# Holding four vector sums behind a named sum, and another tile for one raw weight load, in a hybrid decoder layer

## The chip, the cores and the metric

The kernel runs on one core of a Trainium2 chip. The metric is the device time of one execution in microseconds (us); the median of the runs counts. TensorE (PE) multiplies, VectorE (DVE), ScalarE (ACT) and GpSimd (POOL) work on tiles, and transfers are issued from the queues of SyncE (SP) and of POOL. All products are single-precision, each made of three matmuls in fp32r over a high and a low half of both operands.

## The reference

One layer on 1024 tokens of width 1024. `r = x + mix(norm(x)) @ w_out`, where the mix is three groups of heads (a gated recurrence, a sliding window attention, a retention). Then the gated MLP with inner width 2816,

```
h2 = rmsnorm(r) * ffn_norm
gate = causal_conv3(h2 @ w_gate) + conv_b
r = r + (gelu(gate) * (h2 @ w_up)) @ w_down
r = r + (p @ w_ple_proj) * sigmoid((rmsnorm(r) * ple_norm) @ w_ple_gate)
out = rmsnorm(r) * final_norm
```

## The kernel before, in words

The attention part comes first (to about 400 us). It ends with the last gated heads, whose columns are scaled by the first norm, held in the tile `rs1` (tag `rs`, one buffer, in the pool that lives through the whole kernel). Then come the output projection and the projection of `p` (tiles `pp`), to 508 us.

The MLP's two products with `h2` are done in 22 *units* of 128 inner columns by a seven-product scheme (Strassen in Winograd's form): each unit needs products 1 to 7 instead of eight, on sums of quarters of the weights and of `h2`. One product is four blocks of three matmuls, twelve in all. `weights_up_1(f)` loads a unit's raw gate weights `wg` (512 KB, SP queue) and splits them into a high half (ACT, `whig`) and a low half (DVE, `wlog`); `weights_up_2(f)` loads the raw up weights `wu` and makes the sums `s12`, `f34`, `f4` with their halves. `Unit.early` makes products 1 and 2; for units 0, 1 and 2 these run before anything else, since they need only the plain `h2`. `Unit.rest` makes the others. It keeps three banks: `a` (product 2), `d` (5, then 3 on top) and `b` (1, 6, 7 and 4, one on top of the other). Between the products DVE and ACT read a bank before the next product adds to it: after product 7 `plus(u1, "b")` (L942, `us<-gb,us`) must have read bank `b` before product 4 writes it, with product 3 between; after product 3 `plus(g1, "d")` (L942, `gs<-gd,gs`) starts the convolution (L945 on ACT, L946 and L948 on DVE) on the tiles `gs` and `cv`, one buffer each.

Unit outputs go to DRAM from the POOL queue: an even unit stores `he` (L990), an odd one `ta`, `ho` and `tb` (L997 to L1001). `sent[f]` is the store after which `sums_down` may issue its load.

The down product is a seven-product scheme too. Its weight sums are made in 22 *pieces*, by `sums_down(n)`: a load of four 128x256 blocks from `w_dn` into tile `sd` (512 KB, POOL queue; tag `rs`, one buffer), four DVE operations (L1010 and three of L876, `sd<-sd`), a store to `s_dram` (POOL queue). Unit f (from 3 on) calls `sums_down(f - 3)`; pieces 19, 20 and 21 follow after the last unit.

The down phase runs seven passes in the order 1, 2, 6, 5, 7, 3, 4 of eleven steps each; a step is twelve matmuls, two steps share a group of raw weights `wdr` and four steps share raw activations `hr` (tag `hx`, six buffers), all loaded from the SP queue. Passes 1, 2 and 4 read `w_dn`, the others read `s_dram`. `residual(i)` loads two tiles of `r` (tag `hx` too, kept to the end); `gate_weights(d)` loads and splits `w_ple_gate` for the stage after it, the first three of them when a pass ends.

A planner orders the instructions of each engine before the run, from dependencies, priorities (`tc.high_priority` moves a block ahead) and estimated durations; on the chip every engine takes its instructions strictly in that order. `tc.issue_after(x)` puts the block's instructions of x's engine behind x in that order, without a wait of its own.

Of the kernel before, what the change touches and what calls it, by code (L numbers as in the profile page):

```python
# [17 lines left out]
F32 = mybir.dt.float32  # L18
# [4 lines left out]
ALU = mybir.AluOpType  # L23
# [3 lines left out]
P = 128  # L27
T = 1024
# [3 lines left out]
NF = 22  # L32
# [4 lines left out]
NJ = NF // 2  # L37
# [36 lines left out]
def trunk(ctx: ExitStack, tc: tile.TileContext, a, out, dbg):  # L74
    nc = tc.nc
    V, S, G, TE = nc.vector, nc.scalar, nc.gpsimd, nc.tensor

    cp = ctx.enter_context(tc.tile_pool(name="const", bufs=1))
# [14 lines left out]
    def half(h):  # L93
        return slice(h * H2, (h + 1) * H2)
# [31 lines left out]
    def col(i):  # L126
        return small[:, i:i + 1]
# [74 lines left out]
    with tc.high_priority(offset=100000):  # L202
# [4 lines left out]
        for k in range(KD):  # L207
            x = xs[k]
# [9 lines left out]
            for h in range(2):  # L218
                S.mul(hi[:, half(h)], x[:, half(h)], col(C_G1 + k))
                V.scalar_tensor_tensor(out=lo[:, half(h)], in0=x[:, half(h)], scalar=col(C_G1 + k),  # L220
                                       in1=hi[:, half(h)].bitcast(F32), op0=ALU.mult, op1=ALU.subtract)
# [480 lines left out]
    f, k = hgrn_f(0, first[0])  # L702
# [5 lines left out]
    f, k = got["af1"]  # L708
# [14 lines left out]
    for hd in range(2):  # L723
        r = slice(hd * 64, hd * 64 + 64)
# [33 lines left out]
    def f4(tag, name, shape=(P, T), dt=F32):  # L758
        if tag == "big":
            return big.tile(list(shape), dt, tag="big", name=name)  # L760
        if tag in ("wraw", "whi", "wlo"):
            return wp.tile(list(shape), dt, tag=tag, bufs=1 if tag == "wraw" else 2, name=name)
        return fp.tile(list(shape), dt, tag=tag, bufs=BUFS[tag], name=name)
# [29 lines left out]
    ho_dram, ta_dram, tb_dram = [dp.tile([NJ, P, T], F32, name=n) for n in ("hod", "tad", "tbd")]  # L793
# [3 lines left out]
    r = [f4("r", f"r{d}") for d in range(KD)]  # L797
# [77 lines left out]
    def minus(out, x, y):  # L875
        V.tensor_tensor(out=out, in0=x, in1=y, op=ALU.subtract)  # L876


    def weights_up_1(f):

        g = f4("ws" if f == 2 else "w5" if f > 2 and f % 2 else "wraw", f"wg{f}")
        nc.sync.dma_start(g.rearrange("p (k c) -> p k c", k=KD), a["w_gu"][f, 0])
        hi, lo = [f4(t, f"{t}g{f}", dt=F32R) for t in ("whi", "wlo")]
        hl(hi, lo, g)
        return g, {n + 1: (hi[:, half(n)], lo[:, half(n)]) for n in range(2)}
# [21 lines left out]
    class Unit:  # L907
# [21 lines left out]
        def rest(self):  # L929
            f, bank = self.f, self.bank  # L930
            gs, cv, us = [f4(t, f"{t}{f}") for t in ("gs", "cv", "us")]
            g0, g1 = [gs[:, half(i)] for i in range(2)]
            u0, u1 = [us[:, half(i)] for i in range(2)]

            def w(j):
                return col(C_CW + 3 * f + j)

            def copy(out, to):
                S.copy(out, bank[to])  # L939

            def plus(out, to):
                V.tensor_tensor(out=out, in0=bank[to], in1=out, op=ALU.add)  # L942

            def conv():
                S.activation(cv, gs, AF.Identity, bias=col(C_CB + f), scale=w(2))  # L945
                V.scalar_tensor_tensor(out=cv[:, 1:], in0=gs[:, :T - 1], scalar=w(1), in1=cv[:, 1:],  # L946
                                       op0=ALU.mult, op1=ALU.add)
                V.scalar_tensor_tensor(out=cv[:, 2:], in0=gs[:, :T - 2], scalar=w(0), in1=cv[:, 2:],  # L948
                                       op0=ALU.mult, op1=ALU.add)
                S.activation(cv, cv, AF.Gelu_apprx_tanh)  # L950

            if f < 3:
                copy(g0, "b")
                plus(g0, "a")
            if f == 0:
                self.prod(5)
                copy(u1, "d")
                self.prod(3)
                copy(g1, "d")
                self.prod(6)  # L960
                plus(g1, "b")
                conv()
                self.prod(7)
                plus(u1, "b")
            else:
                if f > 2:
                    s1 = fp.tile([P, H2], F32, tag="s1", bufs=1, name=f"s1{f}")
                    self.prod(1)
                    copy(s1, "b")
                    self.prod(5)  # L970
                    copy(u1, "d")
                self.prod(6)
                copy(g1, "b")
                if f > 2:
                    self.prod(2)
                    V.tensor_tensor(out=g0, in0=bank["a"], in1=s1, op=ALU.add)
                else:
                    self.prod(5)
                    copy(u1, "d")
                self.prod(7)  # L980
                plus(u1, "b")
                self.prod(3)
                plus(g1, "d")
                conv()
            self.prod(4)
            V.tensor_tensor(out=u0, in0=bank["b"], in1=cv[:, half(0)], op=ALU.mult)
            V.tensor_tensor(out=u1, in0=u1, in1=cv[:, half(1)], op=ALU.mult)
            j = f // 2
            if f % 2 == 0:
                sent[f] = G.dma_start(he_dram[j], u1)  # L990
                even.append(us)
                return
            e0, e1 = [even[j][:, half(i)] for i in range(2)]
            t1, t2 = [cv[:, half(i)] for i in range(2)]
            minus(t1, e0, e1)
            minus(t2, u0, t1)
            G.dma_start(ta_dram[j], cv)  # L997
            minus(e0, u0, e0)
            minus(e1, u1, t2)
            G.dma_start(ho_dram[j], us)  # L1000
            sent[f] = G.dma_start(tb_dram[j], even[j])  # L1001

    def sums_down(n):

        j, c = n // 2, slice(n % 2 * 256, n % 2 * 256 + 256)
        t = cp.tile([P, 4, 256], F32, tag="rs", bufs=1, name=f"sd{n}")
        with tc.issue_after(sent[min(n + 2, NF - 1)].ins):
            G.dma_start(t, a["w_dn"][:, j, :, c].rearrange("b p c -> p b c"))
        a11, a12, a21, a22 = [t[:, i, :] for i in range(4)]
        V.tensor_tensor(out=a22, in0=a21, in1=a22, op=ALU.add)  # L1010
        minus(a21, a11, a21)
        minus(a11, a22, a11)
        minus(a12, a12, a11)
        G.dma_start(s_dram[:, j, :, c].rearrange("b p c -> p b c"), t)

    even, sent = [], {}
# [34 lines left out]
    for f in range(3, NF):  # L1051
        with tc.high_priority(offset=3000):
            raw, A = weights_up_1(f)
            weights_up_2(f, raw, A)
        sums_down(f - 3)
        Unit(f, A).rest()


    for n in range(NF - 3, NF):
        sums_down(n)  # L1060
    steps = [(i, j) for i in DOWN for j in range(NJ)]
    raws = {}

# [33 lines left out]
    r = [None] * KD  # L1097
# [5 lines left out]
    def residual(i):  # L1103

        t = f4("hx", f"rr{i}", (P, 2, T))
        for d in (2 * i, 2 * i + 1):
            r[d] = t[:, d % 2, :]
            nc.sync.dma_start(r[d], r_dram[d])
        r2.append(t)
# [25 lines left out]
    def gate_weights(d):  # L1135
        with tc.high_priority(offset=300 if d > 2 else 0):
            raw = f4("us" if d < 3 else "ws" if d % 2 else "wraw", f"wpg{d}")
            nc.sync.dma_start(raw.rearrange("p (k c) -> p k c", k=KD), a["w_pg"][d])
            tags = ("whi", "wlo") if d in (3, 4) else ("big", "big")
            hi, lo = [f4(t, f"{c}pg{d}", dt=F32R) for t, c in zip(tags, "hl")]  # L1140
            hl(hi, lo, raw)
            wpg[d] = [x.rearrange("p (k c) -> p k c", k=KD) for x in (hi, lo)]
# [5 lines left out]
    bank = {}  # L1148
    todo = []
    for n, (i, j) in enumerate(steps):  # L1150
        if n % 2 == 0:
            got[n // 2] = parts(n // 2)
        if n in (4, 6, 12, 15):
            residual((4, 6, 12, 15).index(n))
        if n > 5 * NJ and todo or todo and j % 2:
            done(*todo.pop(0))
        (wh, wl), (xh, xl) = got[n // 2]
        to = "y" if i in (2, 5, 3) else "x"
        new = i in (1, 2, 5)
        if new and j == 0:  # L1160
            bank[to] = [(pg if (d < 2 if to == "y" else d == 0) else b1)(f"d{i}{d}") for d in range(4)]
        for d in range(4):
            mm3(bank[to][d], wh[:, n % 2, d * P:d * P + P], wl[:, n % 2, d * P:d * P + P], xh[:, n % 2, :],
                xl[:, n % 2, :], new and j == 0, j == NJ - 1, not new)
        if j == NJ - 1:
            d0, h = TO[i]
            for d in range(4):
                V.tensor_tensor(out=r[d0 + d][:, half(h)], in0=bank[to][d], in1=r[d0 + d][:, half(h)], op=ALU.add)
            if i in DONE:
                todo += [(DONE[i][0] + d, DONE[i][1]) for d in range(4)]  # L1170
            if i in (2, 6, 5):
                gate_weights((2, 6, 5).index(i))
    for x in todo:
        done(*x)
    for d in range(3, KD):
# [174 lines left out]
```

## Time and profile before

| | us |
|---|---|
| three runs | 1269.79, 1271.68, 1275.17 |
| median | 1271.68 |
| profiled execution, its span | 1272.79, 1270.8 |
| PE busy, DVE busy, ACT busy | 1236.2, 903.2, 551.7 |
| matmuls | 6198 |
| MLP units, about | 508 to 952 |
| down phase, about | 952 to 1160 |

The profiled execution is one of the program's executions; its span runs from the first to the last instruction. An idle stretch is shown in brackets with what ended it. The granted clock of TensorE is 1.00 at 2.4 GHz and 0.50 at 1.2 GHz; a mean between them says that a stretch had both.

### The profile page before, as it was taken

The numbers are of one execution on the slowest core, as the hardware profiler recorded it, in microseconds if no ns is written. First come the engines' busy times: TensorE is split into PE (matmuls) and PEld (weight loads), VectorE is DVE, ScalarE is ACT, GpSimd is POOL, SyncE is SP. The second block draws the span as 40 slices with busy tenths as digits, with TensorE's granted clock in tenths as the row PEclk, the third lists the DMA queues.
The fourth block names the chain that finished last, engine by engine and source line by source line (L and its number), as shares of the span: only waits on it lengthen the run. The fifth ranks groups of instructions, "written<-read, shape, count | busy, mean of one in ns | idle before, by whom it ended". The sixth has DMA issues, their size and how long they took to land. (4 is left out here: it accounts for less than half of the span.)

```text
span 1270.8 us, 16249 instructions
## 1 busy us (share of the span) xinstructions
PE 1236.2 (97%) x6198; PEld 1034.7 (81%) x6198; DVE 903.2 (71%) x1563; ACT 551.7 (43%) x856; POOL 130.2 (10%) x162
## 2 busy tenths in 40 slices
PE   9999999999999999999999999999999999999996
PEld 7888888888888888778787888888778778888896
DVE  7986967566776387787878778778573765665676
ACT  7324233248675355444433433343352343543432
POOL 2000000012210332000111110111101000000010
PEclk9999999999999999999999999999999999999998
DMA  7110110110103844223555444454689664543132
GB/s 253 50 32 19 34 34 18 34 50 18 34 18 104 311 133 158 91 92 124 186 179 166 154 170 132 158 174 156 217 289 348 227 235 162 164 139 100 42 109 83
DMA packets 61021, 165.02 MB, mean 130 GB/s; under 512 B 6096, under 2 KB 8656, under 8 KB 60944
## 3 DMA queue, kind: packets, MB, share of 16 engines
q1 hardware_dynamic: 43744, 106.44, 25.1%
q0 software_dynamic: 15616, 55.84, 12.9%
q10 hardware_dynamic: 1584, 1.71, 0.5%
q8 instruction: 48, 0.79, 0.2%
q14 instruction: 29, 0.24, 0.1%
HBM read 119.67 MB, written 44.30 MB: 129 GB/s over the span
## 5 line engine op out<-in xcount | busy, mean ns | idle before, releaser
L115 PE MATMUL d<-hhd,hwd 128*128 128x512 f32 x308 | 120.5, 391 | 2.5 <-ACT hwd L770 2.5
L117 PE MATMUL d<-hhd,lwd 128*128 128x512 f32 x308 | 120.8, 392 | 1.1 <-DVE lwd L771 1.1
L116 PE MATMUL d<-lhd,hwd 128*128 128x512 f32 x308 | 120.4, 391 | 0.0
L771 DVE TENSOR_TENSOR lwd<-wdr,hwd 128x1024 fp32r<-128x1024 f32 (+1 forms) x39 | 47.0, 1209 | 44.0 <-ACT hwd L770 43.9
L115 PE MATMUL gb<-b,hf 128*128 128x512 f32 x176 | 70.1, 399 | 5.6 <-DVE us L942 4.5
L770 ACT CAST hwd<-wdr 128x1024 fp32r<-128x1024 f32 (+1 forms) x39 | 40.3, 1038 | 78.7 <-PE d L116 63.5
L115 PEld LDWEIGHTS d<-hhd,hwd 128*128 128x128 f32 x308 | 58.2, 189 | 14.9 <-ACT hwd L770 2.9
L117 PE MATMUL gd<-b,f 128*128 128x512 f32 x176 | 68.3, 390 | 1.5 <-DVE f L771 1.5
L117 PEld LDWEIGHTS d<-hhd,lwd 128*128 128x128 f32 x308 | 58.2, 189 | 13.9 <-DVE lwd L771 1.9
L115 PE MATMUL gd<-b,f 128*128 128x512 f32 x176 | 68.8, 391 | 0.4 <-ACT us L939 0.2
L116 PE MATMUL gb<-b,hf 128*128 128x512 f32 x176 | 68.7, 390 | 0.0
L117 PE MATMUL gb<-b,lf 128*128 128x512 f32 x176 | 68.7, 390 | 0.0
L116 PE MATMUL gd<-b,f 128*128 128x512 f32 x176 | 68.5, 389 | 0.0
L116 PEld LDWEIGHTS d<-lhd,hwd 128*128 128x128 f32 x308 | 58.1, 189 | 12.1
L115 PE MATMUL pg<-hp,hpg 128*128 128x256 f32 (+1 forms) x192 | 61.7, 322 | 0.0
L116 PE MATMUL pg<-lp,hpg 128*128 128x256 f32 (+1 forms) x192 | 61.4, 320 | 0.0
L117 PE MATMUL pg<-hp,lpg 128*128 128x256 f32 (+1 forms) x192 | 61.2, 319 | 0.0
L770 ACT CAST hhd<-hr 128x1024 fp32r<-128x1024 f32 (+1 forms) x39 | 39.8, 1035 | 33.5 <-DMA hr<-tad 17.9
L771 DVE TENSOR_TENSOR lhd<-hr,hhd 128x1024 fp32r<-128x1024 f32 (+1 forms) x39 | 46.5, 1206 | 8.0 <-ACT hhd L770 7.8
L771 DVE TENSOR_TENSOR f<-s,f 128x1024 fp32r<-128x1024 f32 x22 | 26.9, 1225 | 33.5 <-ACT f L770 33.4
L770 ACT CAST f<-wg 128x512 fp32r<-128x512 f32 x22 | 13.7, 623 | 84.0 <-PE gd L117 84.0
L115 PEld LDWEIGHTS gb<-b,hf 128*128 128x128 f32 x176 | 33.0, 188 | 17.4 <-DVE us L942 7.7
(459 smaller groups left out, 3501.3 us busy)
## 6 DMA issues: line engine op xcount, KB each, us to landing
wu<-w_gu SPq DMA_DIRECT2D x22, 512.0 KB, 3.5
wg<-w_gu SPq DMA_DIRECT2D x22, 512.0 KB, 3.7
sd<-w_dn POOLq DMA_DIRECT2D x22, 512.0 KB, 5.2
sd<-sd POOLq DMA_DIRECT2D x22, 512.0 KB, 3.9
wdr<-sd SPq DMA_DIRECT2D x20, 512.0 KB, 4.2
wr_wo<-w_out SPq DMA_DIRECT2D x16, 512.0 KB, 3.7
wdr<-w_dn SPq DMA_DIRECT2D x15, 512.0 KB, 4.6
hod<-us POOLq DMA_DIRECT2D x11, 512.0 KB, 2.9
```

Source lines behind the costliest of these rows:

```text
L115: TE.matmul(o, wh, xh, start=first, stop=False, skip_group_check=on)
L116: TE.matmul(o, wh, xl, start=False, stop=False, skip_group_check=on)
L117: TE.matmul(o, wl, xh, start=False, stop=last, skip_group_check=on)
L770: S.copy(hi, src)
L771: e.tensor_tensor(out=lo, in0=src, in1=hi.bitcast(F32), op=ALU.subtract)
```

## The change

Unit 1's raw gate weights go to a tile with tag `rs` instead of `wraw`. `plus` returns its instruction; units 1 to 21 call `sums_down(f - 1, ...)` with the instruction of `plus(u1, "b")`, and the four DVE operations stand behind it in DVE's order. The load of piece n is issued after `sent[n]` instead of `sent[n + 2]`. The last piece, 21, is called at the end of the first pass of the down phase, behind the last addition to `r` there. An odd unit's `sent` is now the store of `ho` and not the one of `tb`. `residual` 1, 2 and 3 move from steps 6, 12 and 15 to steps 7, 22 and 26, and the first three `gate_weights` from the ends of passes 2, 6, 5 to those of 6, 5, 7.

```diff
 def weights_up_1(f):
-        g = f4("ws" if f == 2 else "w5" if f > 2 and f % 2 else "wraw", f"wg{f}")
+        if f == 1:
+            g = cp.tile([P, T], F32, tag="rs", bufs=1, name="wg1")
+        else:
+            g = f4("ws" if f == 2 else "w5" if f > 2 and f % 2 else "wraw", f"wg{f}")
...
                 self.prod(7)
-                plus(u1, "b")
+                sums_down(f - 1, plus(u1, "b"))
                 self.prod(3)
                 plus(g1, "d")
                 conv()
...
-            G.dma_start(ho_dram[j], us)
-            sent[f] = G.dma_start(tb_dram[j], even[j])
+            sent[f] = G.dma_start(ho_dram[j], us)
+            G.dma_start(tb_dram[j], even[j])
...
-    def sums_down(n):
+    def sums_down(n, after):
...
-        with tc.issue_after(sent[min(n + 2, NF - 1)].ins):
+        with tc.issue_after(sent[n].ins):
             G.dma_start(t, a["w_dn"][:, j, :, c].rearrange("b p c -> p b c"))
...
-        V.tensor_tensor(out=a22, in0=a21, in1=a22, op=ALU.add)
-        minus(a21, a11, a21)
-        minus(a11, a22, a11)
-        minus(a12, a12, a11)
+        with tc.issue_after(after.ins):
+            V.tensor_tensor(out=a22, in0=a21, in1=a22, op=ALU.add)
+            minus(a21, a11, a21)
+            minus(a11, a22, a11)
+            minus(a12, a12, a11)
         G.dma_start(s_dram[:, j, :, c].rearrange("b p c -> p b c"), t)
...
-        sums_down(f - 3)
         Unit(f, A).rest()
-    for n in range(NF - 3, NF):
-        sums_down(n)
...
-        if n in (4, 6, 12, 15):
-            residual((4, 6, 12, 15).index(n))
+        if n in (4, 7, 2 * NJ, 2 * NJ + 4):
+            residual((4, 7, 2 * NJ, 2 * NJ + 4).index(n))
...
-                V.tensor_tensor(out=r[d0 + d][:, half(h)], in0=bank[to][d], in1=r[d0 + d][:, half(h)], op=ALU.add)
+                x = V.tensor_tensor(out=r[d0 + d][:, half(h)], in0=bank[to][d], in1=r[d0 + d][:, half(h)], op=ALU.add)
+            if i == 1:
+                sums_down(NF - 1, x)
...
-            if i in (2, 6, 5):
-                gate_weights((2, 6, 5).index(i))
+            if i in (6, 5, 7):
+                gate_weights((6, 5, 7).index(i))
```

## Rows read from the trace of the kernel before

**Rows 1.** The first part of the page: busy time of each engine, its share of the span, instructions.

```profile
PE 1236.2 (97%) x6198; PEld 1034.7 (81%) x6198; DVE 903.2 (71%) x1563; ACT 551.7 (43%) x856; POOL 130.2 (10%) x162
```

**Rows 2.** The table by stretches: length; busy time of PE, its weight loads, DVE, ACT, POOL; granted clock; busy share of the DMA engines; GB/s. The stretches are the first half of the output projection, the preparation of the first units, units 0 to 2, the units in their steady run, the last two units, the first two passes.

```profile
400.00:450.00 50.00, 50.00 (x226) 41.30 (x225) 23.56 (x37) 16.37 (x20) 12.78 (x14) 1.00 0.76 268
...
489.00:535.00 46.00, 42.87 (x186) 34.88 (x185) 42.07 (x71) 27.32 (x44) 5.00 (x7) 0.96 0.38 133
535.00:600.00 65.00, 62.92 (x271) 50.00 (x270) 48.35 (x63) 28.58 (x34) 3.47 (x6) 1.00 0.36 114
...
700.00:900.00 200.00, 199.35 (x877) 164.02 (x876) 156.51 (x219) 78.52 (x93) 26.80 (x41) 1.00 0.47 154
900.00:960.00 60.00, 57.22 (x251) 46.75 (x251) 42.65 (x52) 26.13 (x29) 7.59 (x12) 1.00 0.83 296
960.00:1010.00 50.00, 49.46 (x219) 40.65 (x218) 25.39 (x32) 16.17 (x17) 3.79 (x5) 1.00 0.74 265
```

**Rows 3.** Who PE waited for between 420 and 1160 us, all of it: waiting line and what it waited for, us in total, times, longest.

```profile
PE gb L115 <- DVE us L942: 4.5, 4, 1.4
PE gb L115 <- ACT whig L770: 3.0, 1, 3.0
PE d L115 <- ACT hwd L770: 2.5, 1, 2.5
PE gd L117 <- DVE f L771: 1.5, 1, 1.5
PE d L117 <- DVE lwd L771: 1.1, 2, 0.5
PE gb L115 <- ACT gs L939: 0.7, 2, 0.5
PE gb L115 <- DVE gs L942: 0.4, 1, 0.4
PE gd L115 <- ACT us L939: 0.2, 1, 0.2
```

**Rows 4.** The timeline of PE around 517 us (start, duration), and the table by stretches for five us of it.

```profile
514.47 0.39 PE L117 MATMUL gb<-b,f 128*128 128x512 f32 x1
517.90 0.79 PE L115 MATMUL gb<-b,whig 128*128 128x512 f32 x1 [3.05 <-ACT whig L770]
...
521.19 0.39 PE L117 MATMUL gb<-b,wlog 128*128 128x512 f32 x1
...
515.00:520.00 5.00, 2.10 (x5) 1.71 (x6) 2.77 (x4) 2.51 (x3) 0.00 (x0) 0.74 0.06 24
```

**Rows 5.** The timelines of DVE, SP and ACT: the last reader of `rs1`, the last reader of unit 0's raw gate weights, the load of unit 1's, and the cast that waits for it.

```profile
384.05 0.68 DVE L281 TENSOR_TENSOR cg<-z_cg,rs 128x512 f32<-128x512 f32 x1
508.93 0.69 DVE L771 TENSOR_TENSOR f<-wg,f 128x512 fp32r<-128x512 f32 x1
509.65 0.33 SPq L882 DMA_DIRECT2D wg<-w_gu  x1
516.80 1.99 ACT L770 CAST whig<-wg 128x1024 fp32r<-128x1024 f32 x2 [2.56 <-DMA wg<-w_gu]
```

**Rows 6.** The tile `sd` by operation (duration in ns, least, median, most; first and last start), and DVE's waits for it between 540 and 1000 us.

```profile
L876 DVE TENSOR_TENSOR sd<-sd x66: 415/424/427, 600.3 to 1003.6; 128x256 f32<-128x256 f32 x66
DVE sd L1010 <- DMA sd<-w_dn: 32.8, 14, 10.2
```

**Rows 7.** The timelines of DVE and PE in one unit: the sums of a piece, the two `plus`, and product 3's first and last matmul with the first of product 4.

```profile
664.69 0.42 DVE L1010 TENSOR_TENSOR sd<-sd 128x256 f32<-128x256 f32 x1 [1.75 <-DMA sd<-w_dn]
668.16 0.42 DVE L876 TENSOR_TENSOR sd<-sd 128x256 f32<-128x256 f32 x1
669.10 0.69 DVE L942 TENSOR_TENSOR us<-gb,us 128x512 f32<-128x512 f32 x1
665.87 0.39 PE L115 MATMUL gd<-b,f 128*128 128x512 f32 x1
668.37 0.39 PE L117 MATMUL gd<-b,f 128*128 128x512 f32 x1
669.84 0.50 PE L115 MATMUL gb<-b,hf 128*128 128x512 f32 x1 [1.08 <-DVE us L942]
```

**Rows 8.** The chain of waits that ended last, in order of time (start, us, what), around 1000 us, and the timeline of PE there.

```profile
993.09 8.00 DMA sd<-w_dn
1001.21 0.42 DVE sd L1010
1008.59 0.36 SPq L1075
1009.00 8.31 DMA wdr<-sd
...
1015.55 0.39 PE L117 MATMUL d<-hhd,lwd 128*128 128x512 f32 x1
1018.43 0.50 PE L115 MATMUL d<-hhd,hwd 128*128 128x512 f32 x1 [2.49 <-ACT hwd L770]
1022.73 0.40 PE L115 MATMUL d<-hhd,hwd 128*128 128x512 f32 x1
```

**Rows 9.** The timelines of DVE and ACT: the last operation of a unit's convolution on DVE, and the next unit's write to the same tile `gs`.

```profile
654.17 1.28 DVE L948 SCALAR_TENSOR_TENSOR cv<-gs,small,cv 128x1022 f32<-128x1022 f32 x1
661.59 0.58 ACT L939 COPY gs<-gb 128x512 f32<-128x512 f32 x1
```

More of the change, by code (lines that the diff above doesn't have):

```diff
@@ L941, in plus @@
             def plus(out, to):
-                V.tensor_tensor(out=out, in0=bank[to], in1=out, op=ALU.add)
+                return V.tensor_tensor(out=out, in0=bank[to], in1=out, op=ALU.add)
             def conv():
```

## The prediction

> **What bounds the kernel now.** I began with the busy times: PE has work in 97% of the span [rows 1], so the other engines matter only where PE stands still, and of the 34.6 us in which it does (1270.8 less 1236.2) I had to find those that the change can touch. The list of PE's waits over the MLP and down phases answers that [rows 3]: eight lines, 13.9 us together. They fall into four places. First, unit 1's gate weights (`whig`), 3.05 us in one piece. Second, a matmul of bank `d` that waited for the low half of `f12`, 1.5 us, with a 0.4 beside it. Third, the units: 4.5 us in four pieces for `plus(u1, "b")`, and 0.7 and 0.2 us for copies to `gs` and `us`. Fourth, the down phase: 2.5 us for `hwd` and 1.1 us for `lwd`.
>
> Behind the first and the fourth come matmuls at the lower clock. In steady work a matmul starts 0.227 us after the one before: product 3 has eleven such steps in 2.50 us [rows 7]. From 514.47 to 521.19 us there are nine steps, which would take 2.04 us and took 6.72 [rows 4]: a loss of 4.7 us, 3.1 of it idle and 1.5 of it slow matmuls, with a mean granted clock of 0.74 in five us of it (1.2 GHz for a part, 2.4 for the rest). From 1015.55 to 1022.73 us, ten steps took 7.18 us instead of 2.27 [rows 8]: 4.9 us, and with the other half of the `lwd` waits 5.5.
>
> So the ceiling of the whole change is 4.7 + 1.9 + 5.4 + 5.5 = 17.5 us, 1.4% of the time.
>
> **Part 1, unit 1's raw gate weights.** Before, they shared the tile `wraw` with unit 0's. The last reader of unit 0's runs on DVE until 509.62 us, the load is issued at 509.65, and it has landed when ACT's cast starts at 516.80 [rows 5]. PE waits for this cast. In the tile `rs` the load can go once `rs1` has had its last reader, at 384.73 us [rows 5], 125 us earlier. The cast then hangs on its own slot (two tiles `whi`, of which the projection of p holds one until its last matmul, just before 508.57), so I put it at about 509 to 510 us and the low half at about 511, with PE asking for both at 514.7. The wait goes with its slow matmuls: 4.7 us.
>
> What is late next: DVE, which has 42.07 us of work in the 46 us up to 535 [rows 2]. It is idle for 3.9 us there, part of it for the same cast, so it can get earlier by at most that, and PE by 4.7. PE has 72 matmuls of products 1 and 2 ahead, 16 us from 508.57 at 0.227 each, before it needs the forms of `h2` that DVE is making, so these are not in the way at once; but the wait for `f12` (1.5 us, rows 3) stays and may grow. I take 0.5 back: 4.2 us gained, bounds 2.0 (DVE gains half of its idle time and paces PE from there) and 4.7.
>
> The load itself (512 KB) moves ahead of other loads in SP's queue. If it runs at about 385 us, loads of the output weights and of the residual stand behind it; PE was never idle from 400 to 450 us, though the DMA engines were 76% busy [rows 2], so they have room. Zero, with a bound of 1.8 us if it lands among them (512 KB at 296 GB/s, the fullest stretch of rows 2).
>
> **Part 2, the sums behind `plus(u1, "b")`.** A piece has four DVE operations of 0.42 us [rows 6], 1.7 us together; their number, 22, does not change. What changes is their place. In the unit of rows 7 DVE waited 1.75 us for the transfer, with all else behind it, and then did the four among other work; bank `b` was ready when product 3 began at 665.87, and `plus(u1)` ran only at 669.10, after product 3's last matmul at 668.37. So product 4 began 1.1 us late. Behind `plus`, the sums can't delay it. In all DVE waited 32.8 us for such loads, 14 times [rows 6].
>
> After the change: `plus(u1)` at about 666.1, its 0.69 us and 1.7 us of sums end at 668.5, and `plus(g1)` can start only at about 668.7, when product 3 is through. So the sums fit between the two. Their data must be there by 666.8; in that unit it was there at 664.69, and the load is issued at the same store as before (unit f now loads f - 1 after `sent[f - 1]`; before it loaded f - 3 after the same store). In the last two units the DMA engines are 83% busy [rows 2]; a piece took 8.0 us when the queues were full [rows 8], and such a load may land some 2 us after `plus(u1)`. DVE would then wait with the convolution behind it. That has room: DVE's part of it ends at 655.45 us, and the next unit writes `gs` at 661.59 [rows 9], 6.1 us later.
>
> Of the 5.4 us in the units I take 4.0: the 4.5 us for `plus` less half of the longest of them (1.4, in the last unit, where halves for the down phase also stand ahead of `plus`), 3.8, and a quarter of the 0.9 for copies, 0.2; bounds 0 and 5.4. Against it stand the sums 0 and 1, which now come in units 1 and 2, where DVE has 48.35 us of work in 65 and PE has waited for it [rows 2, 3]: between 0 and 3.4 us (twice 1.7), and I take 1.0, since the idle DVE time of 16.7 us in that stretch is five times what is added.
>
> On POOL's queue the load of a piece is now issued before an odd unit's store of `tb`. It waits until the store of the piece before has emptied the tile; `tb` waits behind it, and it is read only in passes 7 and 4. Zero.
>
> **Part 3, the down phase.** Before, pieces 19 to 21 made a chain of their own in the one tile `sd`. The chain of waits shows its end [rows 8]: the load of the last piece starts at 993.09 and takes 8.00 us, DVE waits for it until 1001.21 with the halves `lhd` and `lwd` behind it; so the tiles `hx` come free late, SP's queue, which is in order, issues at 1008.59, and the `wdr` load behind it starts at 1009.00 and takes 8.31 us. PE waits for its cast. With the change pieces 19 and 20 are done in units 20 and 21, piece 21 loads beside the first pass, and its sums stand behind that pass's last addition; none of them holds DVE. Two residual loads (2 MB) and the first gate weights leave the stretch around 940 to 1000 us, where the DMA engines are 74 to 83% busy [rows 2], and two more tiles `hx` serve `hr` until step 22. Both links of the chain are cut, so I take 5.0 of the 5.5 us. The residuals and gate weights don't vanish: they come at steps 22 and 26 and 30 us later, on SP's queue among the loads of passes 6 and 5, with only two `hx` left for `hr` then, as before. If one load is late there, PE pays a stall like this one, 5.5 us; if none, zero; I take 0.5, a chance of about one in ten.
>
> **A rule weighed.** In these rows the slow matmuls behind the two long waits cost about 1.5 us each, some seven steps longer by 0.2 us (512 columns at 1.2 instead of 2.4 GHz). The Trainium skill, TensorE: Matmul & The Clock Gate, section "What's actually happening", holds that the number of slow matmuls behind a cold start is not fixed: the same kernel had 6, 11 or 14 of them in different runs. By that rule an estimate of the clock's part is 6 to 14 matmuls of 0.2 us extra, 1.2 to 2.8 us a stall, and the sum would be 11.1 to 14.3 us by it where rows give 11.7; the trace agrees with its lower end.
>
> **Sum.** 4.2 + 4.0 - 1.0 + 5.0 - 0.5 = 11.7 us. The profiled execution took 1272.79 us (2.0 us around its span), which gives 1261.1; it lies 1.1 us above the median of the runs, so the median should come to 1260.0.
>
> **The rivals.**
> (a) Only a part arrives. The planner makes a new order for every engine, and a queue that was one wait late may be late at the next: SP's at steps 22 to 30, where residuals take two `hx` back. For it: the loads are moved and not removed, and there is no spare transfer time in 940 to 1010. Against it: the stretch after it is less loaded. Then part 3 gives nothing: 1271.7 less 6.7 is 1265.0, or with half of the units' waits kept, 1267.
> (b) The change does nothing that can be measured: the waits of the units are traded for others in DVE's order, and the clock and DMA waits fall elsewhere. 4.2 us for the first wait, against 1 to 4 us lost in the others: 1268 to 1271. For it: 13.9 us of waiting in 740 us is little, and PE is at 97% already.
> (c) Slower. The four sums delay `plus(g1)` and with it the convolution; if DVE is behind by more than the 6.1 us of room [rows 9], the one tile `gs` is not free when the next unit copies to it, and PE waits in every unit. Price 1.7 us times 21 units, 36 us gross, 24 net: 1296; if only units 1 to 10 lag, 17 gross and 5 net: 1277. For it: two waits for `gs` exist already (0.7 us, rows 3). Against it: in the steady run DVE has 156.5 us of work in 200 [rows 2], so it catches up 4 us in every unit of 19.
> The threshold of this measurement is 0.5%, 6.4 us, so "faster" means below 1265.3.
>
> **How the numbers follow.** The forecast 0.57, (a) 0.20, (b) 0.14, (c) 0.09. Nearly all of the first and a quarter of (a) are faster; the rest of (a) and (b) are no change; (c) is slower by over 0.5% in about two thirds of its cases. That gives 0.61, 0.33 and 0.06. The range goes from the ceiling (1271.7 less 17.5, 1254) to 1269, which takes in (a) and the better half of (b).
>
> **What would show it.** In the changed kernel's trace: no wait of PE for `whig` near 517 us and a clock of 1.00 there; the load of `wg1` before 508 us; no wait of DVE for `sd` loads of over 2 us and the four sums right behind `us<-gb,us` in every unit; PE's waits for `plus(u1)` below 1 us in total; no wait for `hwd` near 1018 us; POOL issuing the last `sd` load before 965 us. I am wrong on part 1 if PE waits at the same place for another tile, on part 2 if `gs` or `us` waits rise above 2 us, on part 3 if a wait for `hwd`, `hhd` or their low halves of 2 us or more appears later in the down phase.

## The result: 7 us of the 11.7 forecast

The changed kernel takes 1263.88 us (median of 4 runs, 1263.71 to 1264.40). The kernel before took 1270.89 beside it (4 runs, 1269.79 to 1275.17). The ratio is 0.9939 [0.9916, 0.9963], which is about 7.8 us. The profiled executions differ by 8.7 us in span (1270.8 and 1262.1). The forecast was 1260.0 us, with a range of 1254 to 1269: the side and the range held. Of the 11.7 us, 7.0 arrived by the medians, 7.8 by the ratio and 8.7 by the spans, so about a third is missing.

Its place shows when the same matmul is found in both traces. The lead of the changed kernel at six points (start times in us):

| matmul | before | after | lead |
|---|---|---|---|
| first of the units' products | 508.57 | 508.51 | 0.1 |
| product of unit 1 behind the `f12` waits | 554.91 | 548.91 | 6.0 |
| product 3 in the unit of [rows 7] | 665.87 | 661.86 | 4.0 |
| last of product 3 in unit 21 | 939.55 | 931.27 | 8.3 |
| first of the down phase | 944.23 | 941.31 | 2.9 |
| first behind the down phase (`pg`) | 1159.44 | 1150.79 | 8.7 |

Between the first row and the second the trace has 169 matmuls of the changed kernel and 172 of the kernel before, in another order; three steps of 0.227 us are 0.7, so of the 6.0 us 5.3 were won. From the third row on the counts agree. So the stretch of the first wait gave 5.3 us, the units up to the one of [rows 7] took 1.3 back, those from there to the last gave 4.3, the last unit took 5.4 back, and the down phase gave 5.7. Behind it nothing changed.

First the page's busy times, to be held against [rows 1]:

```profile
PE 1233.6 (98%) x6198; PEld 1034.8 (82%) x6198; DVE 906.5 (72%) x1563; ACT 552.1 (44%) x856; POOL 130.3 (10%) x162
```

Then who PE waited for from 420 to 1160 us, as in [rows 3]: us in total, times, longest.

```profile
PE gb L115 <- DVE us L945: 5.6, 2, 4.5
PE gd L117 <- DVE f L771: 0.7, 1, 0.7
PE gb L115 <- ACT gs L942: 0.7, 2, 0.4
PE gd L115 <- ACT f L770: 0.6, 1, 0.6
PE gd L115 <- ACT us L942: 0.4, 1, 0.4
```

The lines for `whig`, `hwd` and `lwd` are gone. The line for `plus(u1)`, which the sums were to leave free, is larger than before: 5.6 us in two pieces instead of 4.5 in four (L945 is the old L942). The table by stretches, with the columns of [rows 2] and [rows 4], says where they lie:

```profile
489.00:535.00 46.00, 45.88 (x205) 37.40 (x205) 44.00 (x74) 29.39 (x47) 5.01 (x7) 1.00 0.43 144
...
515.00:520.00 5.00, 5.00 (x24) 4.14 (x23) 4.99 (x8) 2.84 (x5) 0.00 (x0) 1.00 0.04 18
...
700.00:900.00 200.00, 200.00 (x885) 165.62 (x884) 160.50 (x223) 80.40 (x95) 26.80 (x41) 1.00 0.50 159
900.00:960.00 60.00, 55.53 (x234) 45.18 (x233) 40.60 (x49) 24.68 (x27) 7.60 (x12) 0.94 0.84 296
...
935.00:940.00 5.00, 3.87 (x9) 3.11 (x10) 4.04 (x8) 2.19 (x2) 0.75 (x1) 0.50 1.00 371
960.00:1010.00 50.00, 50.00 (x222) 41.43 (x221) 30.77 (x34) 21.50 (x23) 0.76 (x1) 1.00 0.76 272
```

PE is busy without a gap at 515, in the steady run and in the first passes. In 900 to 960 us it works less than before (55.53 instead of 57.22) and at a lower mean clock (0.94 instead of 1.00). Around 937 us half of the full clock was granted: 1.2 GHz.

The timeline of PE (start, duration, what, and the idle time before it with its releaser) shows the new wait in unit 1 and the last unit's:

```profile
557.34 0.50 PE L115 MATMUL gb<-b,hf 128*128 128x512 f32 x1 [1.14 <-DVE us L945]
...
931.27 0.39 PE L117 MATMUL gd<-b,f 128*128 128x512 f32 x1
936.13 0.80 PE L115 MATMUL gb<-b,hf 128*128 128x512 f32 x1 [4.47 <-DVE us L945]
...
940.99 0.48 PE L117 MATMUL gb<-b,lf 128*128 128x512 f32 x1
941.31 0.39 PE L115 MATMUL d<-hhd,hwd 128*128 128x512 f32 x1
```

From 931.27 to 941.31 there are thirteen steps, 2.95 us at 0.227 each. They took 10.04: 7.1 us lost, 4.5 of it idle, most of the rest in twelve matmuls at half the clock (the last of them in part). Before, the same two product ends lay at 939.55 and 944.23, 4.68 us, of which 1.7 were lost. That is the 5.4.

Why `plus(u1)` was late there is told by the chain of waits that ended last, in order of time (start, us, what):

```profile
904.56 7.76 DMA sd<-w_dn
912.41 0.44 DVE sd L1014
...
914.13 0.69 DVE gs L945
...
919.84 0.09 ACT s L942
...
920.30 1.06 ACT hhd L770
...
922.53 1.23 DVE lhd L771
923.78 8.23 DMA hr<-hed
932.04 1.05 ACT hhd L770
933.11 0.98 DVE lhd L771
...
934.26 1.22 DVE lhd L771
935.48 0.61 DVE us L945
936.13 0.80 PE gb L115
```

To be read from the end. Product 4 waits for `plus(u1)` (`us`, 935.48). On DVE that stands behind two halves `lhd` for the down phase (933.11, 934.26). These need a cast of `hr`. Its load of 1 MB took 8.23 us and could start only at 923.78, when DVE had made the halves before it and a tile became free. Those stand behind unit 20's convolution, behind its `plus(g1)` (914.13), and behind the four sums, which had waited 2.0 us for their load (912.41). The halves aren't needed before the down phase, but DVE takes its work in order.

In the kernel before, the same order stood, with the same halves ahead. Its timelines of PE, DVE, SP and ACT, the first line from unit 20:

```profile
920.59 0.50 PE L115 MATMUL gb<-b,hf 128*128 128x512 f32 x1 [1.34 <-DVE us L942]
...
928.50 2.36 DVE L771 TENSOR_TENSOR lhd<-hr,hhd 128x1024 fp32r<-128x1024 f32 x2
930.89 0.38 SPq L1075 DMA_DIRECT2D hr<-hed  x1
937.27 2.00 ACT L770 CAST hhd<-hr 128x1024 fp32r<-128x1024 f32 x2 [1.91 <-DMA hr<-hed]
941.37 0.50 PE L115 MATMUL gb<-b,hf 128*128 128x512 f32 x1 [1.44 <-DVE us L942]
```

There the load took 6.4 us from its issue, and PE came to product 4 only 8.9 us after it (939.78, a step behind 939.55). In the changed kernel the load took 8.2 us and PE came 7.7 us after it (931.50). So the wait grew by 1.8 us of slower transfer and 1.2 us of an earlier PE. PE no longer stood 1.34 us for `plus(u1)` in unit 20. At the end of product 3 it was 8.3 us ahead of the kernel before, and the issue of this load only 7.1 us (923.78 against 930.89).

### The profile page after: what moved, and what is told of

Read it like the earlier page. It is cut to its first block, busy times and chain, and to the rows that moved or that the text cites. A ratio compares the mean times of both kernels' runs of the same rounds, so it can differ in the third digit from the quotient of the medians.

```text
span 1262.1 us, 16241 instructions
## 1 busy us (share of the span) xinstructions
PE 1233.6 (98%) x6198; PEld 1034.8 (82%) x6198; DVE 906.5 (72%) x1563; ACT 552.1 (44%) x856; POOL 130.3 (10%) x162
## 4 chain that ended last, share of the span: by engine, by line
PE 69%; DVE 7%; DMA 3%; ACT 2%; issue 2%; POOL 1%; DVEq 0%; ACTq 0%; POOLq 0%
PE d L116 6%; PE d L115 6%; PE d L117 6%; PE gb L115 5%; PE gb L116 5%; PE gb L117 5%; PE pg L115 2%; PE pg L117 2%; PE pg L116 2%; PE o L115 2%; PE o L117 2%; PE o L116 2%; PE gd L117 2%; PE gd L116 2%; PE gd L115 2%
## 5 line engine op out<-in xcount | busy, mean ns | idle before, releaser
L771 DVE TENSOR_TENSOR lhd<-hr,hhd 128x1024 fp32r<-128x1024 f32 (+1 forms) x39 | 46.7, 1205 | 11.7 <-ACT hhd L770 11.5
```

What stands on the lines that cost most here:

```text
L771: e.tensor_tensor(out=lo, in0=src, in1=hi.bitcast(F32), op=ALU.subtract)
```

## The experiments

Ratios are to the kernel before, with 95% intervals.

| run | median us | ratio |
|---|---|---|
| after | 1263.88 | 0.9939 [0.9916, 0.9963] |
| e1_hold | 1257.21 | 0.9889 [0.9873, 0.9905] |
| e2_resid_late | 1263.59 | 0.9946 [0.9925, 0.9966] |
| e3_wg1_alone | 1265.95 | 0.9953 [0.9933, 0.9974] |
| e4_no_wg1 | 1267.99 | 0.9974 [0.9961, 0.9988] |
| e5_resid_old | 1265.70 | 0.9958 [0.9945, 0.9972] |
| e6_pieces_old | 1266.03 | 0.9963 [0.9951, 0.9974] |
| e7_no_pin | 1265.94 | 0.9968 [0.9953, 0.9983] |
| e9_hold_swap | 1256.52 | 0.9891 [0.9873, 0.9909] |
| e10_sums_alone | 1268.02 | 0.9967 [0.9951, 0.9983] |

### Is it the order on DVE? (e1_hold)

The changed kernel, with the two halves put behind the last unit's `plus(u1)`; nothing else differs.

```diff
-                sums_down(f - 1, plus(u1, "b"))
+                held.append(plus(u1, "b"))
+                sums_down(f - 1, held[-1])
...
-                hl(hi[:, :n], lo[:, :n], raw[:, :n])
+                if len(got) == 1 and g in (2, 3):
+                    with tc.issue_after(held[-1].ins):
+                        hl(hi[:, :n], lo[:, :n], raw[:, :n])
+                else:
+                    hl(hi[:, :n], lo[:, :n], raw[:, :n])
```

> The changed kernel, with the low halves of the activations of groups 2 and 3 put behind the last unit's plus(u1) in DVE's order; nothing is left out. Theory (the order of DVE): in the changed kernel PE stands still for 4.47 us at 931.7 to 936.1 us only because plus(u1) stands behind these two halves, whose transfer lands at 932; with them behind it the wait and its 12 matmuls at half the clock go, 7.1 us together, and the time is about 1257 us. Rival (PE would wait for the next thing, the convolution or the halves of the down phase, which wait for the same transfers): 1261 to 1264 us, and a new wait of 2 us or more between 930 and 960 us.

Measured: 1257.21 us, 6.7 below the changed kernel; the two intervals don't overlap. The timelines of PE and DVE in the last unit:

```profile
932.50 0.39 PE L117 MATMUL gd<-b,f 128*128 128x512 f32 x1
932.73 0.39 PE L115 MATMUL gb<-b,hf 128*128 128x512 f32 x1
...
930.21 0.69 DVE L945 TENSOR_TENSOR us<-gb,us 128x512 f32<-128x512 f32 x1 [0.63 <-PE gb L117]
934.08 2.36 DVE L771 TENSOR_TENSOR lhd<-hr,hhd 128x1024 fp32r<-128x1024 f32 x2 [3.18 <-ACT hhd L770]
```

Product 4 follows product 3 one step later, without idle time. DVE does `plus(u1)` at once and then waits 3.18 us for the same cast, where nobody on PE waits for it. Up to this point both traces have the instructions of every engine in the same order, but for `plus(u1)` on DVE; only behind it three more on DVE, one cast on ACT and one load on POOL changed places. So this run shows the order as the cause.

### Or the loads around it? (e2_resid_late)

The changed kernel, with the first two residuals one and four steps later.

```diff
-        if n in (4, 7, 2 * NJ, 2 * NJ + 4):
-            residual((4, 7, 2 * NJ, 2 * NJ + 4).index(n))
+        if n in (8, 9, 2 * NJ, 2 * NJ + 4):
+            residual((8, 9, 2 * NJ, 2 * NJ + 4).index(n))
```

> The changed kernel, with the first two residual loads at steps 8 and 9 instead of 4 and 7. Theory (the order of DVE): plus(u1) of the last unit still stands behind the same two halves; the transfer they wait for shares the engines with other loads that move up, so the wait stays between 2.5 and 5 us and the time between 1261 and 1265 us. Rival (the two residual loads issued right behind it make this transfer slow): without them 1 MB lands in 5 us or less instead of 8.2, the wait falls below 1.5 us, and the time to 1257 to 1259 us.

Measured: 1263.59 us, nothing gained. SP's issues and the timeline of PE:

```profile
922.63 0.93 SPq L1076 DMA_DIRECT2D hr<-hed  x2
...
934.84 0.79 PE L115 MATMUL gb<-b,hf 128*128 128x512 f32 x1 [4.33 <-DVE us L945]
```

The wait stayed, and `hr` took 8.1 us, as in the changed kernel: SP issued two loads of `hr` together, in the time that the residuals had left. So the residuals as such are not the cause of the wait, but what a load alone would take there was not isolated: of the 1.8 us of slower transfer only the size is known, not the neighbour it came from.

### The new tile, alone and taken away (e3_wg1_alone, e4_no_wg1)

e3 is the kernel before with only unit 1's raw weights in the tile `rs`; e4 is the changed kernel with this undone.

```diff
-        g = f4("ws" if f == 2 else "w5" if f > 2 and f % 2 else "wraw", f"wg{f}")
+        if f == 1:
+            g = cp.tile([P, T], F32, tag="rs", bufs=1, name="wg1")
+        else:
+            g = f4("ws" if f == 2 else "w5" if f > 2 and f % 2 else "wraw", f"wg{f}")
```

> The kernel before with the tile of unit 1's raw gate weights alone changed. Theory (the parts add up): the wait for whig at 517 us and its slow matmuls go, 4.7 us, and the waits in the units and at 1018 us stay: about 1266 us. Rival (the planner's new order moves the other waits): within 2 us of the kernel before, or below 1263, with other waits in the units or in the down phase.

> The changed kernel with unit 1's raw gate weights in their old tile. Theory (the parts add up): the wait for whig comes back, and the time is 4.7 us above the changed kernel's 1263.9, about 1268.6. Rival (the rest of the change does the work): within 1.5 us of 1263.9.

Measured: e3 1265.95 us, e4 1267.99. PE's waits in e3 from 420 to 1160 us:

```profile
PE gb L115 <- DVE us L945: 5.6, 5, 3.3
PE d L115 <- ACT hwd L770: 1.2, 1, 1.2
```

The timeline of PE in e4:

```profile
517.02 0.50 PE L115 MATMUL gb<-b,whig 128*128 128x512 f32 x1 [2.46 <-ACT whig L770]
...
939.78 0.80 PE L115 MATMUL gb<-b,hf 128*128 128x512 f32 x1 [3.93 <-DVE us L942]
```

Without the tile the wait for `whig` is back and the time is 4.1 us above the changed kernel. The tile alone gives 5.2 by the medians of its series (before: 1271.18). But a part of it comes back even alone: in e3 the last unit's wait grew from 1.44 to 3.3 us.

### The sums alone and left out (e10_sums_alone, e6_pieces_old)

e10 is the kernel before with only the sums moved; e6 is the changed kernel with the sums where they were before.

```diff
 e10, against the changed kernel
-        if f == 1:
-            g = cp.tile([P, T], F32, tag="rs", bufs=1, name="wg1")
...
-        if n in (4, 7, 2 * NJ, 2 * NJ + 4):
+        if n in (4, 6, 12, 15):
...
-            if i in (6, 5, 7):
+            if i in (2, 6, 5):
 e6, against the changed kernel
-                sums_down(f - 1, plus(u1, "b"))
+                plus(u1, "b")
...
+        sums_down(f - 3)
         Unit(f, A).rest()
```

> The kernel before with the sums alone moved (calls, order and loads as in the changed kernel; unit 1's weights, residual loads and gate weights as before). Theory (the sums clear the units from 600 to 930 us, 3.1 us, and the down phase, 5.5 us, and the last unit's wait behind the two low halves grows by about 5.5): the waits for whig at 517 and for plus(u1) in the last unit stand, none over 0.5 us in the down phase, and the time is 1266 to 1269 us, 2 to 4.5 below the kernel before. Rival (the last unit's wait comes from the earlier start that the new tile gives): no wait over 2 us in the last unit, and 1263 us or less.

> The kernel before with unit 1's weights in the new tile and with the moved residual loads and gate weights, but the sums as before. Theory (the sums in the tail hold DVE and with it the tiles hx): the waits in the units stay and one near 1015 us, and the time is 1264 to 1267 us, about that of the new tile alone (1266.0). Rival (the moved loads clear the down phase): no wait of over 0.5 us in the down phase, and 1262 us or less.

Measured: e10 1268.02 us (before in that series: 1272.07), e6 1266.03. In e10 PE has no wait left in the down phase, and none for `plus(u1)` in the middle units; the last unit's wait is 3.91 us, with no new tile in the kernel. In e6 the waits are the other way about. Its timelines of DVE and PE:

```profile
915.47 0.43 DVE L1013 TENSOR_TENSOR sd<-sd 128x256 f32<-128x256 f32 x1 [4.81 <-DMA sd<-w_dn]
...
917.01 0.50 PE L115 MATMUL gb<-b,hf 128*128 128x512 f32 x1 [3.04 <-DVE us L945]
938.20 0.50 PE L115 MATMUL gb<-b,hf 128*128 128x512 f32 x1 [0.23 <-DVE us L945]
```

In unit 20 DVE stands 4.81 us for a piece with `plus(u1)` behind it, and PE pays 3.04; then the last unit costs 0.23. A wait of PE in unit 20 and one in unit 21 replace each other, though not to the same sum: 1.34 and 1.44 us before, 0.54 and 3.31 in e3, 3.04 and 0.23 in e6, none and 4.47 in the changed kernel. In these runs a PE that came earlier, without DVE's halves coming earlier by as much, paid for it in the last unit.

### The edge on the sums, and the moved loads (e7_no_pin, e5_resid_old)

e7 lets the planner put the sums where it likes, with the new call and the new load time kept; e5 gives residuals and gate weights their old steps.

```diff
 e7
-        with tc.issue_after(after.ins):
+        if True:
 e5
-        if n in (4, 7, 2 * NJ, 2 * NJ + 4):
+        if n in (4, 6, 12, 15):
...
-            if i in (6, 5, 7):
+            if i in (2, 6, 5):
```

> The changed kernel without the order of the four sums behind plus(u1) and behind the last addition of the first pass; calls and loads stay where they are. Theory (the order is what frees product 4): the planner puts sums ahead of plus(u1) in some units, PE waits there again for 0.5 to 1.5 us each, 2 to 4 us in all, and the time is 1265 to 1268 us. Rival (the later place of the calls and the earlier pieces do it): within 1 us of 1263.9, and no new waits for plus(u1).

> The changed kernel with the residual loads (steps 4, 6, 12, 15) and the first gate weights (after passes 2, 6, 5) at their old places. Theory (the down phase is clear because no sum holds DVE there): no wait for hwd near 1010 us comes back, and the time is within 2 us of the changed kernel's 1263.9. Rival (the moved loads cleared it): a wait of 2 us or more in the down phase, and 1266 us or more.

Measured: e7 1265.94 us, e5 1265.70. PE's waits in e7:

```profile
PE gb L115 <- DVE us L945: 5.9, 4, 2.9
```

The four lie at 558.39 (1.14), 665.92 (0.24), 915.65 (1.57) and 937.93 (2.95). In the middle units only 0.24 us came back, so the earlier load and call did most there and the edge little; my expectation of waits in several units was wrong. In e5 PE has no wait in the down phase either, so the moved loads are not what cleared it. Both runs lie some 2 us above the changed kernel, with intervals that overlap: what the edge and the moved loads are worth, between 0 and about 2 us each, stays open.

### Unit 1's wait as well (e9_hold_swap)

e1_hold, with the two tiles of the raw gate weights exchanged between odd and even units from unit 3 on. In the changed kernel DVE had stood 4.15 us for unit 3's load, with unit 1's `plus(u1)` behind it; its timeline of DVE:

```profile
550.78 0.69 DVE L876 TENSOR_TENSOR wu<-wg,wu 128x512 f32<-128x512 f32 x1 [4.15 <-DMA wg<-w_gu]
...
556.60 0.68 DVE L945 TENSOR_TENSOR us<-gb,us 128x512 f32<-128x512 f32 x1
```

The edit:

```diff
-            g = f4("ws" if f == 2 else "w5" if f > 2 and f % 2 else "wraw", f"wg{f}")
+            g = f4("ws" if f == 2 else "w5" if f > 2 and f % 2 == 0 else "wraw", f"wg{f}")
```

> The kernel with the two low halves behind the last plus(u1), and with the tiles of the raw gate weights of units 3 to 21 exchanged (odd units wraw, even ones w5), so that unit 3's load does not wait for unit 0's up weights in w5. Theory (the 1.0 us wait for plus(u1) at 558 us comes from DVE waiting 4 us for unit 3's gate weights): that wait goes, and with it part of the other waits up to 622 us (2.9 us in all): 1255 to 1256.5 us against 1257.2. Rival (DVE is simply late with the first units): the waits stay, 1257 us or more.

Measured: 1256.52 us. The wait at 557 is gone, and the timeline of PE has a new one:

```profile
918.94 0.50 PE L115 MATMUL gb<-b,f 128*128 128x512 f32 x1 [1.92 <-ACT s L942]
```

This is the same pattern on another engine: ACT's copy `s` (918.31) stands there behind two casts for the down phase (`hwd` at 916.41, `hhd` at 917.37). So the cause of the wait at 557 is shown. The time can't be told from e1's: the ratios are 0.9891 and 0.9889. The profiled execution (span 1254.1 us) lies 16.7 below the one of the kernel before, where the ceiling of the forecast was 17.5. Both are faster than the kernel before and the changed one.

## Why the prediction was right, and where it failed

**Part 1 was right.** The load of unit 1's weights was issued at 384.84 us (385 forecast), the cast began at 508.62 and the low half at 510.07 (509 to 510, and 511). The clock in 515 to 520 us is 1.00 instead of 0.74. It won 5.3 us where I had 4.2: the waits behind it, 1.9 us with the one for `f12`, which I let grow by 0.5, fell to 1.4 as DVE came earlier (44.00 us of work in the 46 us where it had 42.07). Taken out again in e4, the part is worth 4.1 us; some of the trace's 5.3 was paid back in the last unit, whose wait is 3.93 us in e4 and 4.47 in the changed kernel.

**Part 2 was right up to unit 20.** In the unit of [rows 7] the sums now stand where I put them; the timeline of DVE in the changed kernel:

```profile
662.07 0.68 DVE L945 TENSOR_TENSOR us<-gb,us 128x512 f32<-128x512 f32 x1
...
663.27 0.41 DVE L1014 TENSOR_TENSOR sd<-sd 128x256 f32<-128x256 f32 x1
663.72 1.34 DVE L876 TENSOR_TENSOR sd<-sd 128x256 f32<-128x256 f32 x3
664.98 0.68 DVE L945 TENSOR_TENSOR gs<-gd,gs 128x512 f32<-128x512 f32 x1
```

They end at 665.06, and `plus(g1)` starts 0.2 us after the end of product 3 (664.74), so it is hardly held. From this unit to product 3 of the last one the lead grew by 4.3 us. DVE still waits for pieces (10.4 us in six waits, the longest 3.1, at 611.44, where I had said none over 2), but in the middle units nobody on PE waits behind it. The units from 1 to this one cost 1.3 us where I took 1.0 for units 1 and 2. But the reason is not the one I gave, the time of two more sums: 1.14 us is the wait at 557.34, behind a load of raw gate weights for which DVE stood 4.15 us.

**The step that failed** is the last unit in part 2: "the 4.5 us for `plus` less half of the longest of them (1.4, in the last unit, where halves for the down phase also stand ahead of `plus`)". I saw the halves in the way and still let half of that wait go. It grew to 4.47 us, with slow matmuls behind it: 5.4 us lost against the kernel before, where I had counted 0.7 gained. That is 6.1 us of difference. Against my terms part 1 gave 1.1 more, the units up to the one of [rows 7] cost 0.3 more, the units behind it gave 1.0 more (4.3 for 3.3) and the down phase 1.2 more; with these, 11.7 becomes 8.6, beside 8.7 measured by the spans. Two of my sentences were too short. "DVE would then wait with the convolution behind it. That has room: DVE's part of it ends at 655.45 us, and the next unit writes `gs` at 661.59 [rows 9], 6.1 us later" looked only at the tile `gs`. Behind the convolution stand also the `s` copy, the cast, the halves, the tile `hx` and SP's load, and they had no room. And I had not asked, for the waits that were to go, what the earlier PE then meets: it met the next entry on DVE, which had moved by less than PE. e1_hold shows that these halves, and not the sums, the tile or the residuals, hold product 4.

**Part 3 was right, and a little more**: 5.7 us against 4.5 (5.0 less 0.5). There is no wait of PE from 960 to 1160 us, POOL issued the last piece's load at 953.20 (before 965), and none came later at steps 22 to 30. e10 and e5 show that the moved sums did it.

**The rivals.** (a) gave 1265 to 1267, near in time but by another way: it let the down phase give nothing, and that phase gave all. (b) is excluded by the interval. (c) did not occur: the waits for `gs` are 0.7 us, as before.

**The rule weighed.** Behind the 4.47 us wait twelve matmuls ran at half the clock, behind the 4.33 us of e2 seven, and behind 3.05 us about seven [rows 4]. This agrees with the Trainium skill, TensorE: Matmul & The Clock Gate, section "What's actually happening", that the count isn't fixed.

## What to carry to other kernels

When a wait is removed, follow the engine that now comes earlier to the next thing that it asks for, and read what stands ahead of that on the other engine's queue. If work for a later phase stands there and itself waits for a load, put it behind, with one edge in the order; here this was worth 6.7 us, nearly as much as the whole change (7.0). Count room for delayed work along every chain that starts behind it, not for the first tile alone.

## What the hardware showed that I had not expected

The clock need not fall at once when PE resumes. In e10, after a wait of 3.91 us, it fell only later; the timeline of PE:

```profile
940.01 0.50 PE L115 MATMUL gb<-b,hf 128*128 128x512 f32 x1 [3.91 <-DVE us L942]
940.35 0.39 PE L116 MATMUL gb<-b,hf 128*128 128x512 f32 x1
...
941.27 0.58 PE L117 MATMUL gb<-b,lf 128*128 128x512 f32 x1
941.65 0.63 PE L115 MATMUL gb<-b,hf 128*128 128x512 f32 x1
```

The first five matmuls ran at the full step (granted clock 1.00 from 940.00 to 941.20), and the slow ones (0.63 instead of 0.39 us, granted clock 0.50 from 941.70 to 944.60) began about 1.3 us after PE had resumed. In the changed kernel the first one behind 4.47 us was slow already, and so was the first one in e4 behind 3.93 us, nearly the wait of e10. So the length of the wait alone doesn't tell when the clock falls. And the same 1 MB load at the same place landed after 5.3 us (e6), 6.4 (before) or 8.2 (after), so a transfer's time read from the kernel before is no constant for the changed one.
